# Tiles at multiples of 64 bytes, weights in block order from the host, float32 head transposes, and a new start of a two-layer diffusion backbone

## The chip, the cores and the metric

The kernel runs on one core of one Trainium2 chip, as one launch. The metric is device time in microseconds; three runs of the kernel before gave 1825.28, 1827.72 and 1827.8 us, the median is 1827.72 us. Beside these runs there is one profiled execution, from which all rows below come. TensorE is called PE, its loads of the stationary operand PEld, VectorE DVE, ScalarE ACT, GpSimd POOL, SyncE SP.

## The reference

Two layers over 256 latent and 256 context tokens of 1024 numbers in float32. Each layer is a half-step SwiGLU, a token mixing, and a half-step SwiGLU again, each with a modulation computed from a conditioning vector:

```python
# per layer; m = c_silu @ w_mod[l] + b_mod[l], nine rows of 1024 (shift, scale, gate of three parts)
h = rms_norm(x) * (1 + scale) + shift
x = x + 0.5 * gate * ((silu(h @ w_gate) * (h @ w_up)) @ w_down)          # D_FF = 2816
x = x + gate * mix(h)      # layer 0: windowed GQA with sink, and differential attention
                           # layer 1: latent attention (C) and 2-D neighbourhood attention (D)
x = x + 0.5 * gate * swiglu(h)
# in the mixings, per head: q, k = rope(rms_norm(q_or_k) * gain); softmax(q @ k.T) @ v
```

The last layer computes its last two parts for the latent tokens alone.

## The kernel before

Everything is kept transposed: `xT[k]` holds 128 channels by 512 tokens. A float32 product is made of three products in the float32r form: each operand is split into a high part and the rest (`split`, lines 97 to 99: an ACT copy and a DVE subtraction), and `mm3` issues hi·hi, hi·lo, lo·hi. In `mm(ps, a, b)` the first operand is the stationary one, the second the moving one.

**The four FFNs** (`ffn`). For each pair of 128-wide slices of D_FF, `wcols` loads 512 KB of weights into `raw`, four 128-row chunks of 256 columns (one row of a chunk is 1 KB in the weight matrix), and splits them into `hs`. The moving operands are `hT[0]` to `hT[7]`, the normed stream, two planes (hi, lo) of 512 tokens each; products land in `gps` and `ups`. Twelve matmuls of 512 columns belong to one slice and four chunks, and one product of gate or up of a pair has 48 in a row: for chunks 0 to 3, then for 4 to 7, both slices. The down projection has `ah` as moving operand and lands in `dps`. The fourth FFN has 258 columns, its moving operand is `hTl` with planes 264 floats apart. `residual` (line 294) adds the result to `xT`. In the last part `emit_out` transposes each finished `xT` on PE (`otp`, line 490), copies it and writes it out.

**The start.** Four tiles `xin` of tokens by channels are loaded, squared on ACT, transposed on PE (32 transposes into `xps`, line 557) to `xT`. `first_loads`, `first_mods` and `first_norm` work in four steps of two `hT` each: 2 MB of `w_mod` into `wm`, 64 matmuls `mps` (line 526; they run in float32, so the trace shows two for each instruction), a transpose `mpt`, then `hT`. The first pair of the first FFN is interleaved with these steps: its 96 matmuls want `hT` in order, and its two halves of weights.

**The mixings** are lists of items whose order is written out (`MIX0`, `MIX1`); a scheduler places the instructions of neighbouring items among each other. Twenty items call `head_rows` (18 with four heads, two with two): it norms and rotates q or k (`head_norm`, result `tk`), splits the result for both token blocks (`hsq`, `sp`), transposes the split heads (`trp`, line 661, 152 in all: per pair of heads four), and copies the result to a tile of 128 by 2 by 256, in which a head's hi part stands in partitions 0 to 63 and its lo part in 64 to 127 (lines 664 and 666). For keys a second tile with the halves exchanged is written (lines 669, 671, 673).

**Addresses.** Small constants share one tile, `const`, of 3636 floats, 14,544 bytes, which is 16 more than a multiple of 64. In the built program `const` itself (identity, ones, `cT`), `hT[0]` and `hT[1]` of the first two FFNs and `hT[0]` to `hT[3]` of the third one begin at multiples of 64 bytes; all other `hT`, every `hs`, `ah`, `hsq`, `tk` and most other tiles that TensorE reads begin 32 bytes behind one. In `hTl` the hi plane is at a multiple, the lo plane 32 behind.

Of the kernel before, what the change touches and what calls it, by code (L numbers as in the profile page):

```python
# [16 lines left out]
P = 128  # L17
# [45 lines left out]
def tile_hybrid_dit(ctx: ExitStack, tc: tile.TileContext, I, out, dbg=None):  # L63
# [74 lines left out]
    def const(name, shape, src=None):  # L138
# [3 lines left out]
        if name not in SHARED:  # L142
            place[name] = at, n
# [21 lines left out]
    bT = const("bT", [P, 2, 9, KC])  # L165
    brow = w2("brow")[:72, :256]
    Q.dma_start(out=brow.rearrange("n (l p) -> n l p", l=2), in_=I["b_mod"].rearrange("l (n p) -> n l p", p=P))

    S.activation(cvec, cvec, AF.Silu)
    cps = bank("tr", "cps")  # L170
    T.transpose(cps[:, :16], cvec, ident[:16, :16])
    for v in range(2):
        V.tensor_copy(cT[:, :, v], cps[:, 8 * v:8 * v + 8])
    bps = bank("tr", "bps")
    for l in range(2):
        T.transpose(bps[:, 72 * l:72 * l + 72], brow[:, l * P:(l + 1) * P], ident[:72, :72])
    V.tensor_copy(bT, bps[:, :144].rearrange("p (l m k) -> p l m k", l=2, m=9))
# [103 lines left out]
    xall = xp.tile([P, KC, NTOK], F32, tag="xT", name="xT")  # L281
    xT = [xall[:, k, :] for k in range(KC)]
# [200 lines left out]
    outs = {}  # L483

    def emit_out(dc):
        if dc % 4 == 0:
            outs["t"] = [w2(f"ot{b}") for b in range(2)]
        for b in range(2):
            pt = bank("tr", "otp")
            T.transpose(pt[:, :P], xT[dc][:, b * P:(b + 1) * P], ident)  # L490
            o = outs["t"][b][:, (dc % 4) * P:(dc % 4 + 1) * P]
            if b:
                S.copy(o, pt[:, :P])
            else:
# [7 lines left out]
    ss0 = const("ss0", [P, 4])
    xin = []
    for tb in range(4):
        t = up.tile([P, D], F32, tag="kq", name=f"xin{tb}", bufs=UNITS["kq"])
        src = I["x"][0] if tb < 2 else I["ctx"][0]
        Q.dma_start(out=t, in_=src[(tb % 2) * P:(tb % 2 + 1) * P, :])
        xin.append(t)


    def first_loads(q):
        tiles = {}
        for k0 in (0, 4):
            for m in (1, 0):
                t = up.tile([P, 4, 256], F32, tag="wm", name="wm", bufs=UNITS["wm"])
                c0 = m * D + 256 * q
                Q.dma_start(out=t, in_=I["w_mod"][0, k0 * P:(k0 + 4) * P, c0:c0 + 256].rearrange("(k p) f -> p k f", p=P))
                tiles[m, k0] = t
        return tiles

    def first_mods(q, tiles):
        ps = bank(("po", "md")[q % 2], "mps")
        for k in range(KC):
            for c in range(4):
                m, x = 1 - c // 2, c % 2
                T.matmul(ps[32 * c:32 * c + 32, :P], cT[:, k, :], tiles[m, k - k % 4][:, k % 4, P * x:P * x + P],  # L526
                         start=(k == 0), stop=(k == KC - 1), tile_position=(0, 32 * c))
        st = w2("mst")[:, :P]
        V.tensor_copy(st, ps[:, :P])
        pt = bank("tr", "mpt")  # L530
        T.transpose(pt[:, :P], st, ident)
        pv = pt[:, :P].rearrange("p (m x r) -> p m x r", m=2, r=32)
        for m in (1, 0):
            for v in range(2):
                add(modT[:, 0, v, m, 2 * q:2 * q + 2], pv[:, 1 - m, :, v], bT[:, 0, m, 2 * q:2 * q + 2])

    def first_norm(q):
        for k in range(2 * q, 2 * q + 2):
# [759 lines left out]
def consts():  # L1298
# [45 lines left out]
```

## Time and profile before

| what | value |
|---|---|
| median of three runs | 1827.72 us |
| profiled execution | 1823.43 us |
| its span, first to last instruction | 1821.4 us |
| mean granted TensorE clock | 0.994 |
| PE busy | 1771.1 us, 97% |
| PEld busy | 1537.0 us, 84% |
| DVE busy | 1219.5 us, 67% |
| ACT busy | 739.6 us, 41% |
| DMA | 256.90 MB, mean 141 GB/s |

A share is an average over stages: the start (0 to 57 us) is full of transfers, the FFNs (57 to 400, 647 to 1391, 1620 to the end) are full of matmuls, the mixings (400 to 647, 1391 to 1620) are where PE waits for other engines.

### The profile page before, as it was taken

How to read it: one execution, taken by the hardware profiler on the slowest of the kernel's cores; microseconds unless marked ns; L12 is line 12 of the kernel's file. 1: busy time of each engine (PE TensorE's matmuls, PEld its weight loads, DVE VectorE, ACT ScalarE, POOL GpSimd, SP SyncE). 2: the span in 40 equal slices, each digit the busy share in tenths (PEclk: the TensorE clock that was granted, in tenths of full speed). 3: DMA queues.
4: the chain of work that ended last, by engine and by line, in shares of the span. 5: the costliest groups of instructions: out<-in, count | busy, mean ns of one | idle time of the engine just before them, and what ended most of it. 6: DMA issues, size and time to landing. Idle time of an engine off the chain costs nothing.

```text
span 1821.4 us, 26782 instructions
## 1 busy us (share of the span) xinstructions
PE 1771.1 (97%) x10563; PEld 1537.0 (84%) x10563; DVE 1219.5 (67%) x2343; ACT 739.6 (41%) x1322; POOL 45.8 (3%) x25
## 2 busy tenths in 40 slices
PE   7999999999999989999999999999999998999999
PEld 5788888898998888888888988888889886789998
DVE  5999953467698699989944633333336688877564
ACT  4333132345666552322322332222234656664442
POOL 0000000011010000000000000000001011000000
PEclk9999999999999999999999999999999999999999
DMA  9877752322110137778943233333233442146552
GB/s 305 274 242 225 236 189 84 116 74 66 50 59 24 51 116 232 242 234 265 337 155 105 82 104 93 95 110 97 76 110 105 85 100 58 58 151 186 185 180 87
DMA packets 214026, 256.90 MB, mean 141 GB/s; under 512 B 21485, under 2 KB 195725, under 8 KB 213901
## 3 DMA queue, kind: packets, MB, share of 16 engines
q1 hardware_dynamic: 213900, 255.19, 45.4%
q8 instruction: 83, 1.36, 0.3%
q14 instruction: 43, 0.34, 0.1%
HBM read 254.11 MB, written 1.05 MB: 140 GB/s over the span
## 4 chain that ended last, share of the span: by engine, by line
PE 86%; DVE 7%; ACT 3%; DMA 2%; issue 1%; SPq 0%; ACTq 0%; DVEq 0%
PE ups L102 24%; PE gps L102 23%; PE dps L102 23%; PE ops L102 3%; PE po L758 2%; PE sc L102 2%; DVE hs L99 1%; DMA bias<-in_d_rpb_dram 1%; PE pdk L102 1%; PE paq L102 1%; PE trp L661 1%; PE ptl L726 1%; PE pdq L102 1%; ACT hs L98 1%; PE mps L526 1%
## 5 line engine op out<-in xcount | busy, mean ns | idle before, releaser
L99 DVE TENSOR_TENSOR hs<-raw,hs 128x1024 fp32r<-128x1024 f32 (+2 forms) x308 | 366.6, 1197 | 258.9 <-ACT hs L98 258.1
L98 ACT ACTIVATE hs<-raw 128x1024 fp32r<-128x1024 f32 (+2 forms) x308 | 314.3, 1030 | 498.2 <-PE dps L102 166.7
L102 PE MATMUL dps<-ah,hs 128*128 128x512 f32 (+1 forms) x2256 | 400.1, 338 | 0.2 <-DVE hs L99 0.2
L102 PEld LDWEIGHTS dps<-ah,hs 128*128 128x128 f32 x2256 | 350.6, 190 | 45.5 <-DVE hs L99 0.4
L102 PE MATMUL gps<-hT,hs 128*128 128x512 f32 (+1 forms) x1680 | 379.8, 382 | 5.6 <-ACT hT L544 2.6
L102 PE MATMUL ups<-hT,hs 128*128 128x512 f32 (+1 forms) x1680 | 377.7, 381 | 0.0
L102 PEld LDWEIGHTS gps<-hT,hs 128*128 128x128 f32 x1680 | 304.1, 189 | 71.0 <-ACT hT L544 3.5
L102 PEld LDWEIGHTS ups<-hT,hs 128*128 128x128 f32 x1680 | 304.6, 189 | 63.4 <-issue 1.0
L211 DVE CUSTOM_DVE_ANT_0 junk<-mraw,cb,const 128x1024 f32<-128x1024 f32 x224 | 283.1, 1281 | 14.0 <-DMA mraw<-in_k_w_modT_dram 8.3
L98 ACT ACTIVATE ah<-af 128x512 fp32r<-128x512 f32 (+1 forms) x88 | 50.5, 575 | 155.1 <-DVE af L92 121.9
L294 DVE SCALAR_TENSOR_TENSOR xT<-dps,const,xT 128x256 f32<-128x256 f32 x112 | 50.2, 478 | 86.2 <-PE dps L102 86.0
L92 DVE TENSOR_TENSOR af<-sg,ups 128x512 f32<-128x512 f32 x66 | 45.2, 685 | 62.5 <-PE ups L102 62.5
L275 POOL TENSOR_TENSOR hs<-raw,hs 128x1024 fp32r<-128x1024 f32 (+2 forms) x21 | 45.6, 2173 | 1566.0 <-ACT hs L274 1500.6
L430 ACT ACTIVATE sg<-gps 128x512 f32<-128x512 f32 x66 | 39.0, 591 | 91.4 <-PE gps L102 91.4
L102 PE MATMUL gps<-hTl,hs 128*128 128x258 f32 x528 | 66.8, 284 | 1.8 <-DVE hTl L375 1.0
L102 PEld LDWEIGHTS gps<-hTl,hs 128*128 128x128 f32 x528 | 64.7, 190 | 2.6 <-DVE hTl L375 1.2
L102 PE MATMUL ups<-hTl,hs 128*128 128x258 f32 x528 | 65.5, 283 | 0.0
L102 PEld LDWEIGHTS ups<-hTl,hs 128*128 128x128 f32 x528 | 64.4, 190 | 0.0
L99 DVE TENSOR_TENSOR ah<-af,ah 128x512 fp32r<-128x512 f32 (+1 forms) x88 | 54.5, 620 | 13.3 <-ACT ah L98 13.3
L686 DVE TENSOR_REDUCE nm<-sc 128x1 f32<-128x512 f32 (+1 forms) x80 | 53.8, 682 | 5.1 <-PE sc L102 4.8
L692 ACT ACTIVATE pr<-sc,nm 128x512 f32<-128x512 f32 (+1 forms) x64 | 40.4, 635 | 18.6 <-DVE nm L686 16.6
L303 ACT ACTIVATE sq<-xT 128x256 f32<-128x256 f32 (+1 forms) x54 | 24.0, 450 | 53.5 <-DVE xT L294 53.0
(296 smaller groups left out, 1892.5 us busy)
## 6 DMA issues: line engine op xcount, KB each, us to landing
mraw<-in_k_w_modT_dram SPq DMA_DIRECT2D x128, 512.0 KB, 4.7
raw<-in_ffn_w_gate_dram SPq DMA_DIRECT2D x88, 512.0 KB, 4.8
raw<-in_ffn_w_up_dram SPq DMA_DIRECT2D x88, 512.0 KB, 4.3
raw<-in_ffn_w_down_dram SPq DMA_DIRECT2D x80, 512.0 KB, 3.6
raw<-in_cd_w_in_dram SPq DMA_DIRECT2D x18, 512.0 KB, 3.9
wm<-in_w_mod_dram SPq DMA_DIRECT2D x16, 512.0 KB, 8.9
raw<-in_ab_w_in_dram SPq DMA_DIRECT2D x16, 512.0 KB, 3.7
raw<-in_ffn_w_down_dram SPq DMA_DIRECT2D x16, 256.0 KB, 2.8
```

What stands on the lines that cost most here:

```text
L92: V.tensor_tensor(out=out_, in0=a, in1=b, op=ALU.mult)
L98: S.activation(h, src, AF.Copy)
L99: V.tensor_tensor(out=l, in0=src, in1=h.bitcast(F32), op=ALU.subtract)
L102: T.matmul(ps, a, b, start=start, stop=stop)
L211: V.tensor_tensor_reduce(out=junk, in0=raw, in1=mod_c[v], scale=0.5 if m in (2, 8) else 1.0, scalar=bT[:, l, m, k:k + 1], op0=ALU.mult, op ...
L275: nc.gpsimd.tensor_tensor(out=hs[:, 1, :n], in0=raw[:, :n], in1=hs[:, 0, :n].bitcast(F32), op=ALU.subtract)
L294: V.scalar_tensor_tensor(out=xT[dc][:, a:e], in0=ps[:, a:e], scalar=modT[:, l, v, m, dc:dc + 1], in1=xT[dc][:, a:e], op0=ALU.mult, op1=ALU ...
L303: S.activation(sq[:, cols], xT[dc][:, cols], AF.Square)
L430: S.activation(sg, g[:, :ntok], AF.Silu)
L686: V.tensor_reduce(out=nm[:, c], in_=view, axis=AX.X, op=ALU.max, negate=True)
L692: S.activation(p[:, cols], sc[:, cols], AF.Exp, bias=nm[:, i + b:i + b + 1], accum_out=den[:, i + b:i + b + 1])
L758: T.matmul(po[64 * x:64 * x + 64, q], val(x, c), pts[x][c], start=c == order[0], stop=c == order[-1], tile_position=(0, 64 * x))
```

## The change

Operands: `const` slots are rounded up to 16 floats, the tile has 3808 floats (15,232 bytes, 238 times 64), and the planes of `hTl` are 272 floats apart. In the built program every operand that TensorE reads then begins at a multiple of 64 bytes.

Layout: the host hands over the stream and the conditioning transposed, `b_mod` transposed, the FFN weights, `ab_w_in`, `ab_w_out`, `cd_w_out` and the first two rows of `w_mod` in blocks, so that a partition's part of a 512 KB load is one run of 4 KB. `cd_w_in`, `w_uq`, `w_ukv` stay. The output is written transposed from `xT`, and the host turns it.

Start: no `xin`, no `xps`; squares are taken from `xT` and summed on DVE; the modulation comes in five steps (one, one, two, two, two `hT`), and all loads of `w_mod` are issued ahead of the second half of the first pair's weights.

Head rows: `tk` is transposed in float32, two heads in one transpose (76 in place of 152), and the split is done behind the transpose: per head an ACT (or DVE) copy of 64 partitions and a DVE subtraction; the exchanged key tile is copied from the first, four copies in place of two.

```diff
-NCONST = 3636
+NCONST = 3808
...
-            place[name] = at, n
+            place[name] = at, -(-n // 16) * 16
...
     def wcols(w, k0, nk, c0, nw, tag=None):
         n = nk * nw
-        src = w[k0 * P:(k0 + nk) * P, c0:c0 + nw].rearrange("(k p) f -> p k f", p=P)
+        if len(w.shape) == 4:
+            assert nw == 256 and c0 % 256 == 0
+            src = w[c0 // 256, :, k0:k0 + nk, :]
+        else:
+            src = w[k0 * P:(k0 + nk) * P, c0:c0 + nw].rearrange("(k p) f -> p k f", p=P)
...
-            hraw.append(hp.tile([P, KC, 2, 264], R32, tag="hTl", name="hTl", bufs=1))
+            hraw.append(hp.tile([P, KC, 2, 272], R32, tag="hTl", name="hTl", bufs=1))
...
     def emit_out(dc):
-        if dc % 4 == 0:
-            outs["t"] = [w2(f"ot{b}") for b in range(2)]
-        for b in range(2):
-            pt = bank("tr", "otp")
-            T.transpose(pt[:, :P], xT[dc][:, b * P:(b + 1) * P], ident)
...
+        Q.dma_start(out=out[dc * P:(dc + 1) * P, :], in_=xT[dc][:, 0:256])
...
+    STEPS = ((0, 1), (1, 1), (2, 2), (4, 2), (6, 2))
+
+    wmall = [up.tile([P, 2, 2, D], F32, tag="wm", name="wm", bufs=4) for _ in range(4)]
...
+    for k in range(KC):
+        if k == 0:
+            S.activation(ssum, xT[k], AF.Square)
+        else:
+            xsq = wmall[3].rearrange("p a m f -> p (a m f)")[:, NTOK * k:NTOK * k + NTOK]
+            S.activation(xsq, xT[k], AF.Square)
+            add(ssum, ssum, xsq)
+    first_mods(*STEPS[0], wms[0])
...
+    def first_steps(b):
+        if b == 0:
+            wms[1:] = [first_loads(*step) for step in STEPS[1:]]
+        for i in ((1, 2), (3, 4))[b]:
+            first_mods(*STEPS[i], wms[i])
+            first_norm(*STEPS[i])
...
     def head_rows(src, v, gain, rope, idm, dst_of, swap_of=None):
...
-            split(spv[:, :, 0, :].bitcast(R32), spv[:, :, 1, :].bitcast(R32), tv[:, b])
-            spf.append(sp)
+        pt = bank("tr", "trp")
         for i in range(nh // 2):
-            pt = bank("tr", "trp")
+            for b in range(2):
+                T.transpose(pt[:, 256 * i + b * P:256 * i + (b + 1) * P], tk[:, (b * nh + 2 * i) * HD:(b * nh + 2 * i + 2) * HD],
+                            idm)
+        for i in range(nh // 2):
+            d = dst_of(i)
             for x in range(2):
-                for b in range(2):
-                    h = 2 * i + x
-                    T.transpose(pt[:, 256 * x + b * P:256 * x + (b + 1) * P], spf[b][:, P * h:P * h + P], idm)
...
+                own, other = (slice(0, 64), slice(64, 128))[::1 - 2 * x]
+                r = pt[own, 256 * i:256 * i + 256]
+                if now[0] in ROWS_DVE.split():
+                    V.tensor_copy(d[own, x], r)
+                else:
+                    S.activation(d[own, x], r, AF.Copy)
+                V.tensor_tensor(out=d[other, x], in0=r, in1=d[own, x].bitcast(F32), op=ALU.subtract)
```

How the scheduler places this, at three places. First the queue of SP at the start of the program, before (a name ending in `_dram` is an input; `wm` is `w_mod`, `raw` an FFN's weights):

```order
L149 DMA const<-in_k_ident_dram 128x128
L167 DMA brow<-in_b_mod_dram 72x2x128
L507 DMA xin_106<-in_ctx_dram 128x1024
L517 DMA wm<-in_w_mod_dram 128x4x256 x4
L268 DMA raw<-in_ffn_w_gate_dram 128x4x256
L268 DMA raw<-in_ffn_w_up_dram 128x4x256
L517 DMA wm<-in_w_mod_dram 128x4x256 x8
L268 DMA raw<-in_ffn_w_gate_dram 128x4x256
L268 DMA raw<-in_ffn_w_up_dram 128x4x256
L517 DMA wm<-in_w_mod_dram 128x4x256 x4
```

and now:

```order
L161 DMA xT<-in_k_xT_dram 128x1024
L493 DMA wm<-in_k_wm_dram 128x1024
L265 DMA raw<-in_k_ffn_w_gate_dram 128x1024
L150 DMA const<-in_k_ident_dram 128x128
L265 DMA raw<-in_k_ffn_w_up_dram 128x1024
L493 DMA wm<-in_k_wm_dram 128x1024 x2
L499 DMA wm<-in_k_wm_dram 128x1024 x12
L265 DMA raw<-in_k_ffn_w_gate_dram 128x1024
L265 DMA raw<-in_k_ffn_w_up_dram 128x1024
L191 DMA cb<-in_c_dram 128x1024
```

The second half of the first pair's weights moved behind the last four of the sixteen loads of `w_mod`; it is now the last of the 24 large transfers of the start.

Second, PE where the first matmul of the FFN stands, before (`nbc` is the norm's broadcast) and now (there it is called `bcs`):

```order
L102 MATMUL nbc<-dg,const 128x128
L526 MATMUL mps<-wm,const 32x128 x16
L102 MATMUL nbc<-dg,const 128x128
L526 MATMUL mps<-wm,const 32x128 x7
L531 MATMUL mpt<-const,mst 128x128
L102 MATMUL gps_472<-hT,hs 128x512
```

```order
L508 MATMUL mps<-wm,const 32x128 x13
L103 MATMUL bcs<-dg,const 128x128 x2
L508 MATMUL mps<-wm,const 32x128 x3
L103 MATMUL bcs<-dg,const 128x128
L514 MATMUL mps<-wm,const 32x128
L103 MATMUL bcs<-dg,const 128x128
L519 MATMUL mpt<-const,mst 128x128
L514 MATMUL mps<-wm,const 32x128 x9
L103 MATMUL gps_423<-hT,hs 128x512
```

Before, the first `gps` stands behind the modulation of the first two `hT`; now it stands behind the first `mps` of the third step too, which read the thirteenth of the 24 transfers.

Third, PE at the first call of `head_rows` in the first mixing (the rows of `bq00`; `pbk` and `pbv` are projections that the scheduler puts around it), before and now:

```order
L102 MATMUL pbk<-hs,hT 128x256 x69
L102 MATMUL pbv<-hw,hT 128x256 x15
L102 MATMUL pbk<-hs,hT 128x256 x2
L102 MATMUL pbv<-hw,hT 128x256
L661 MATMUL trp<-const,hsq 128x128 x2
L102 MATMUL pbv<-hw,hT 128x256
L661 MATMUL trp<-const,sp 128x128
L661 MATMUL trp<-const,hsq 128x128
L661 MATMUL trp<-const,sp 128x128 x2
L661 MATMUL trp<-const,hsq 128x128
L661 MATMUL trp<-const,sp 128x128
```

```order
L103 MATMUL pbk<-hs,hT 128x256 x68
L103 MATMUL pbv<-hw,hT 128x256 x5
L650 MATMUL trp<-const,tk 128x128 x4
L103 MATMUL pbk<-hs,hT 128x256
L103 MATMUL pbv<-hw,hT 128x256 x7
L103 MATMUL pbk<-hs,hT 128x256 x2
```

Eight transposes became four, they read `tk` itself, and they stand some 14 matmuls earlier.

## Rows read from the trace of the kernel before

**Rows 1.** The page: busiest engine, and the chain that ended last, by engine.

```profile
PE 1771.1 (97%) x10563; PEld 1537.0 (84%) x10563; DVE 1219.5 (67%) x2343; ACT 739.6 (41%) x1322; POOL 45.8 (3%) x25
...
PE 86%; DVE 7%; ACT 3%; DMA 2%; issue 1%; SPq 0%; ACTq 0%; DVEq 0%
```

**Rows 2.** PE's groups by shape: line, tiles, count | busy us, mean ns | idle before.

```profile
L102 PE MATMUL gps<-hT,hs 128*128 128x512 f32 x1488 | 351.0, 393 | 3.8 <-ACT hT L544 2.6 <-DVE hs L99 1.2
...
L102 PE MATMUL dps<-ah,hs 128*128 128x512 f32 x1152 | 262.6, 389 | 0.0
...
L490 PE MATMUL otp<-const,xT 128*128 128x128 f32 x16 | 3.7, 290 | 0.5 <-DVE xT L294 0.5
```

**Rows 3.** PE in stretches of the third FFN: length, busy (instructions), clock, DMA.

```profile
1102.29:1107.89 5.60, 5.60 (x25) 1.00 0.31 95
1107.89:1113.37 5.48, 5.48 (x26) 1.00 0.29 86
```

**Rows 4.** PE's timeline in its down projection: start, length, tiles, count.

```profile
1157.69 47.53 PE L102 MATMUL dps<-ah,hs 128*128 128x512 f32 x209
```

**Rows 5.** Stretches before and in the second mixing: length, PE, PEld, DVE, ACT, POOL, clock, DMA.

```profile
1022.22:1025.05 2.83, 2.83 (x26) 2.83 (x25) 2.69 (x5) 0.83 (x2) 0.00 (x0) 1.00 0.61 185
1396.60:1398.02 1.42, 1.42 (x15) 1.42 (x13) 0.59 (x1) 1.22 (x2) 1.42 (x1) 1.00 0.54 186
1398.02:1399.46 1.44, 1.44 (x14) 1.44 (x13) 1.41 (x3) 0.73 (x3) 0.94 (x1) 1.00 0.01 4
```

**Rows 6.** Timeline of PE, ACT and DVE where the second pair begins.

```profile
56.31 1.17 PE L102 MATMUL gps<-hT,hs 128*128 128x512 f32 x4
56.62 1.06 ACT L98 ACTIVATE hs<-raw 128x1024 fp32r<-128x1024 f32 x1
...
57.37 1.22 DVE L99 TENSOR_TENSOR hs<-raw,hs 128x1024 fp32r<-128x1024 f32 x1
58.64 5.60 PE L102 MATMUL gps<-hT,hs 128*128 128x512 f32 x23 [1.16 <-DVE hs L99]
```

**Rows 7.** Stretches with full DMA: 1 KB runs, then mostly 4 KB runs (last columns: share, GB/s).

```profile
2.40:42.00 39.60, 30.81 (x294) 21.63 (x295) 21.23 (x68) 17.67 (x30) 0.00 (x0) 1.00 1.06 345
112.00:116.00 4.00, 4.00 (x19) 3.26 (x18) 3.96 (x7) 1.06 (x1) 0.00 (x0) 1.00 0.98 363
```

**Rows 8.** PE's transposes of one call of head_rows, as a stretch.

```profile
572.46:573.25 0.79, 0.79 (x8) 0.79 (x8) 0.00 (x0) 0.04 (x1) 1.00 0.08 21
```

**Rows 9.** DVE's and ACT's groups of head_rows, and a split out of PSUM.

```profile
L99 DVE TENSOR_TENSOR hsq<-tk,hsq 128x256 fp32r<-128x256 f32 x18 | 8.9, 497 | 1.9 <-ACT hsq L98 1.9
L99 DVE TENSOR_TENSOR sp<-tk,sp 128x256 fp32r<-128x256 f32 x18 | 7.5, 417 | 0.0
...
L99 DVE TENSOR_TENSOR ckt<-cktr,ckt 96x256 fp32r<-96x256 f32 x16 | 6.1, 413 | 0.7 <-ACT ckt L98 0.6
...
L673 DVE CAST dkt<-trp 64x512 fp32r<-64x512 f32 x6 | 4.1, 684 | 4.0 <-ACT dkt L669 4.0
...
L98 ACT ACTIVATE hsq<-tk 128x256 fp32r<-128x256 f32 x18 | 7.5, 414 | 19.4 <-DVE tk L92 9.9 <-DVE tk L95 9.5
```

**Rows 10.** The two mixings as stretches (columns as in the fifth group).

```profile
400.48:647.15 246.67, 237.03 (x1819) 216.94 (x1817) 193.60 (x501) 154.15 (x376) 12.51 (x6) 0.99 0.19 56
1390.88:1619.53 228.65, 212.57 (x1495) 185.13 (x1493) 175.03 (x445) 142.67 (x348) 23.29 (x11) 0.98 0.36 88
```

**Rows 11.** What PE waited for: us in total, times, longest.

```profile
PE trp L661 <- DVE hsq L99: 7.8, 6, 2.5
PE kvt L1109 <- DVE ckv L1105: 4.8, 1, 4.8
```

**Rows 12.** The end: timeline of all engines.

```profile
1817.12 0.48 DVE L294 SCALAR_TENSOR_TENSOR xT<-dps,const,xT 128x256 f32<-128x256 f32 x1 [0.23 <-PE dps L102]
...
1818.14 0.27 ACT L493 COPY ot<-otp 128x128 f32<-128x128 f32 x1 [0.45 <-PE otp L490]
1818.35 0.81 SPq L498 DMA_DIRECT2D out_dram<-ot  x2
```

More of the change, by code (lines that the diff above doesn't have):

```diff
@@ L164, in tile_hybrid_dit @@
     modT = const("modT", [P, 2, 2, 9, KC])
[L165 to L177, printed above, removed]
+    bT = const("bT", [P, 2, 9, KC], I["k_bT"])
+    S.activation(cT[:, :, 0:2], cvec, AF.Silu)
     for m0 in (1, 2):
@@ L502, in tile_hybrid_dit @@
[L502 to L518, printed above, removed]
-        return tiles
@@ L521, in first_mods @@
[L521 to L527, printed above, removed]
+        Q.dma_start(out=out[dc * P:(dc + 1) * P, :], in_=xT[dc][:, 0:256])
+    STEPS = ((0, 1), (1, 1), (2, 2), (4, 2), (6, 2))
@@ new lines, in first_mods @@
+    def first_mods(j, nj, tiles):
+        ps = bank("po", "mps")
+        if nj == 1:
+            for k in range(4):
+                for c in range(4):
+                    T.matmul(ps[32 * c:32 * c + 32, :P], cT[:, k + 4 * (c % 2), :], tiles[1 - c // 2][k + 4 * (c % 2)],
+                             start=(k == 0), stop=(k == 3), tile_position=(0, 32 * c))
+        else:
+            for k in range(KC):
+                for c in range(4):
+                    x = c % 2
+                    T.matmul(ps[32 * c:32 * c + 32, :P], cT[:, k, :], tiles[1 - c // 2][k][:, P * x:P * x + P],
+                             start=(k == 0), stop=(k == KC - 1), tile_position=(0, 32 * c))
@@ L533, in first_mods, with first_norm @@
         for m in (1, 0):
[L534 to L538, printed above, removed]
+            if nj == 1:
+                half = sml(2, "mh")
+                V.tensor_scalar(out=half, in0=pv[:, 1 - m, 0, 0:2], scalar1=bT[:, 0, m, j:j + 1], scalar2=None, op0=ALU.add)
+                add(modT[:, 0, :, m, j], pv[:, 1 - m, 1, 0:2], half)
+            else:
+                for v in range(2):
+                    add(modT[:, 0, v, m, j:j + 2], pv[:, 1 - m, :, v], bT[:, 0, m, j:j + 2])
+    def first_norm(j, nj):
+        for k in range(j, j + nj):
             t = unit("xn", "xn")
@@ L812, in mix0 @@
     def mix0():
-        w_in, w_out = I["ab_w_in"][0], I["ab_w_out"][0]
+        w_in, w_out = I["k_ab_w_in"][0], I["k_ab_w_out"][0]
         tabs = {}
@@ L1267, in w @@
     def w(l, n):
-        return [I[f"ffn{n}_w_{x}"][l] for x in ("gate", "up", "down")]
-    def first_steps(b):
-        for q in ((1, 2), (3,))[b]:
-            first_step(q)
+        return [I[f"k_ffn{n}_w_{x}"][l] for x in ("gate", "up", "down")]
     mixing = [mix0(), mix1()]
@@ L1321, in consts, with laid_out, blocks @@
     return c
-_OUT = (SEQ, D)
+_OUT = (D, SEQ)
+def laid_out(a):
+    import numpy as np
+    a = {k: np.asarray(v) for k, v in a.items()}
+    def blocks(w):
+        n, k, f = w.shape
+        return w.reshape(n, k // P, P, f // 256, 256).transpose(0, 3, 2, 1, 4)
+    c = {"k_xT": np.concatenate([a["x"][0], a["ctx"][0]]).T.reshape(KC, P, NTOK).transpose(1, 0, 2),
+         "k_cT": np.stack([a["c"][0], a["c_ctx"]]).reshape(2, KC, P).transpose(2, 1, 0),
+         "k_bT": a["b_mod"].reshape(2, 9, KC, P).transpose(3, 0, 1, 2),
+         "k_wm1": a["w_mod"][0, :, :2 * D].reshape(KC, P, 2, KC, P)[:, :, :, :2].transpose(3, 2, 1, 0, 4),
+         "k_wm0": a["w_mod"][0, :, :2 * D].reshape(KC, P, 2, 4, 256).transpose(3, 2, 1, 0, 4)}
+    for nm in ("ab_w_in", "ab_w_out", "cd_w_out", *(f"ffn{n}_w_{x}" for n in (1, 2) for x in ("gate", "up", "down"))):
+        c["k_" + nm] = blocks(a[nm])
+    return c
 def kernel(**inputs):
```

115 lines of the change are left out of this document (53 added, 62 removed).

## The prediction

> **What bounds the kernel now.** I read the page first: PE is busy for 97% of the span and holds 86% of the chain that ended last [rows 1]. So a gain must come out of the matmuls themselves, out of the few places where PE waits, or out of the two ends of the program. Then I took PE's groups by shape: most of its time is wide matmuls, 1488 recorded for `gps`, about as many for `ups`, and 1152 for `dps` [rows 2]. Their pace is not one number. In one product of the third FFN the first 24 matmuls read `hT[0]` to `hT[3]`, at a multiple of 64 bytes, against `hs`, 32 bytes behind one, and took 5.60 us; the next 24, both operands at 32, took 5.48 [rows 3], with the clock at 1.00 in both. In a down projection, where `ah` and `hs` are both at 32, 209 took 47.53 us [rows 4]; taking 0.39 us as the length of one [rows 2] off the end, that is (47.53 - 0.39) / 208 = 0.2266 us from start to start. So 24 at the best pace are 5.44 us. Unequal offsets go with 0.16 us more for 24, or 6.8 ns each, and the block behind them with another 0.04. Third, stretches of the mixings, where PE is idle for 246.7 - 237.0 = 9.6 us and 228.7 - 212.6 = 16.1 us [rows 10], and the table of waits for whom it waits. Last, timelines of the two ends.
>
> **Alignment.** If equal offsets are what matters, (0, 0) is as good as (32, 32). A product of the third FFN then gains (5.60 + 5.48) - 2 x 5.44 = 0.20 us; in the first two, half of the unequal matmuls (`hT[0]`, `hT[1]`) gain 0.08 + 0.04 = 0.12. With two products for each of ten full pairs in each FFN: 20 x 0.20 + 40 x 0.12 = 8.8 us. The trace holds no wide product with both operands at a multiple of 64, so this is bounded: 0 if it behaves as now, 8.8 if as (32, 32). I take 8.8, since the blocks differ in nothing that I can see but the offset. At 256 columns the sign is the other way: in the second mixing twelve matmuls with unequal offsets took 1.42 us, the following twelve with equal ones 1.44 [rows 5]; some 670 of the mixings' projections are unequal now, so 670 x 1.7 ns = 1.1 us are lost. Together -7.7.
>
> The Trainium skill, "TensorE: Matmul & The Clock Gate", section "Step-by-step: what each phase is for", says that the moving operand and the weight load have separate read ports and that the next load takes nothing from the running matmul. By that no offset of one against the other should count, and this term would be 0. The rows disagree by 0.12 us in 24 matmuls.
>
> **Start.** The first pair does not wait for PE: with 100 matmuls done at 58.64 us, 96 were done, at 0.227 each, by 57.7 in effect; the wait of 1.16 us before is for the second pair's `hs` [rows 6]. The transfers run at 345 GB/s from 2.4 to 42 us, in runs of 1 KB [rows 7]. Runs of 4 KB, which the FFNs' `mraw` has already, reached 363 [rows 7], so the layout gives 0 to 5% there and I count nothing for it. What shortens the start is order and work: 24 transfers of 0.524 MB and 0.2 MB of small ones are 12.8 MB, in 37.1 us at 345 GB/s, so the last, the second half of the first pair's `up`, lands at 39.5 us (37.7 at 363). ACT's copy of 1.06 and DVE's subtraction of 1.22 us [rows 6] lie behind it, partly under matmuls on `gate`, which lands one transfer earlier (0.524 MB at 345 GB/s, 1.5 us): PE begins the last 48 matmuls near 40.3 and ends them 10.9 us later, at 51.2. Gain: 57.7 - 51.2 = 6.5 us. A wait for the second pair's weights may follow, as now. I take -6, between -3 (a wait of three such) and -8 (363 GB/s).
>
> **Head rows, PE.** Eight transposes take 0.79 us as PE goes through them [rows 8], so 76 fewer save 7.5. The moved split also frees what PE waits for: `trp` waits 7.8 us in six waits for `hsq`, the split [rows 11], and ACT's 0.41 and DVE's 0.50 of it [rows 9] no longer stand ahead of it. Six waits shorter by 0.9 are 5.4; not every release will come that early, since `tk` itself is late, so I take -3 (0 to -5.4).
>
> **Head rows, DVE.** Gone: 36 splits, 8.9 + 7.5 = 16.4 us [rows 9], 0.9 for four of half width, sixteen copies of 0.684 (five of rows, eleven of swaps), 10.9; 28.2 in all. New: 76 subtractions of 256 columns out of PSUM, by the nearest row (`ckt`, 0.413 [rows 9]) 31.4 us; ten row copies at the same price, 4.1; 22 swaps at half of 0.684, 7.5; 43.0 in all. DVE does 14.8 us more, and has 193.6 of 246.7 and 175.0 of 228.7 us full [rows 10]. ACT does less, since the 36 split copies of 0.4 us go and its row copies stay about as long. DVE's new work stands between the transposes and the scores (`sc`), but PE has projections to do in between, and the waits of the mixings that are not from this chain (`kvt`, 4.8 us [rows 11]) stay. Bounds: 0, if projections cover all, to 14.8, if PE waits for each. I take a third, +4.9: the cover is there in the first mixing, and in the second it is thinner. Mixings together: -7.5 - 3 + 4.9 = -5.6.
>
> **Tail.** Sixteen `otp` leave PE: at the pace of the other transposes 1.6 us, a pair by itself takes longer (2 x 0.29 at most [rows 2]), so I take 2.0. Behind the last `residual` (ends 17.60) stood a transpose and a copy, ended at 18.41, before the output's DMA [rows 12]; now the DMA follows directly: 0.8. Together -2.8 (0.8 to 3: all `otp` but the last pair may lie in gaps).
>
> **Sum.** -7.7 - 6 - 5.6 - 2.8 = -22.1 against the profiled execution's 1823.4 gives 1801.3. The median of the runs is 1827.7, higher by a factor of 1.0024; so 1805.5.
>
> **The rivals.** *The offset is not the cause.* Then the alignment term falls to 0, by rows 3 unlikely, as the two blocks differ in the chunk too but nothing else in the trace makes chunks 0 to 3 slower: 1805.5 + 7.7 = 1813. The rule on the two read ports in "TensorE: Matmul & The Clock Gate" of the Trainium skill would lead here. *DVE sets the pace in the mixings.* With DVE at 78% there, the whole 14.8 us lands as waits of `sc` for the rows; for it speaks that the keys' three steps (rows, subtraction, swap) are now in series, against it that PE waits little on this chain now: 1805.5 + 9.9 = 1815. *The multiple of 64 is the slow one, of the other sign.* In all slow blocks the moving operand stood at a multiple of 64. If that alone costs 6.8 ns, the change puts every wide matmul there: 60 products x 48 x 6.8 ns = 19.6 us over the best pace instead of 8.8 now, and 1152 `dps` x 6.8 ns = 7.8. Against the forecast that is 8.8 + 10.8 + 7.8 = 27.4 us: 1833, slower. It decides as soon as the start and the mixings give less than 18.6 us together. Against it speaks that at 256 columns 24 `gps` with the moving `hT[0]` to `hT[3]` at a multiple of 64 took 2.83 us, 118 ns each, no slower than the twelve of the second mixing whose moving `hs` stood at 32 and whose stationary `hT` at 0, 1.42 us [rows 5]. *Better than forecast.* All of the waits for `hsq` go, DVE's work is covered, 4 KB runs hold 363 GB/s: 1805.5 - 2.4 - 4.9 - 2 = 1796, or less where the second pair's waits go as well.
>
> **How the numbers follow.** Forecast 0.55, own range 1796 to 1812; offset not the cause 0.10; DVE 0.19; moving operand at 64 slow 0.07; better 0.09. The range of 1790 to 1820 leaves out the third rival and some of two adding up. About 0.2% (3.7 us) is what a measurement of this kernel can tell from no change; from that, slower 0.06 (the third rival, less the cases where the rest covers it), same 0.07 (its milder form, or the first two rivals with a start that gives nothing), faster 0.87.
>
> **What would show it.** Alignment: in the third FFN both blocks of 24 at 5.44 us, and `dps` unchanged at 0.2266; both at 5.60 and `dps` at 0.2334 would be the third rival. Start: the second pair's `gps` beginning near 52 us. Head rows: 76 `trp` at about 0.1 us, the waits for `hsq` gone; if DVE is the bound, the list of waits shows `sc` released by DVE's subtraction or swap, and the idle time of PE in the mixings grows beyond 26 us. Tail: the last DMA issued right behind the last `xT`. The prediction is wrong if the start's transfers do not hold 345 GB/s, or if the 256-column matmuls change by more than their 1.7 ns, since there are thousands of them.

## The result, and the profile after

The changed kernel takes 1839.47 us (median of four runs, 1838.33 to 1839.88), the kernel before 1827.13 us beside it: a ratio of 1.0069, 95% interval 1.0056 to 1.0082. It is slower by 12.3 us where 22 us less were forecast, and outside the range. The profiled executions differ by 15.2 us in their spans (1836.6 and 1821.4).

First the page of the changed kernel, busiest engines and the chain that ended last, by engine:

```profile
PE 1775.0 (97%) x10445; PEld 1529.0 (83%) x10445; DVE 1243.6 (68%) x2390; ACT 733.1 (40%) x1327; POOL 45.8 (2%) x25
...
PE 83%; DVE 11%; ACT 3%; DMA 1%; issue 1%; SPq 0%; DVEq 0%; ACTq 0%
```

PE's share of the chain fell from 86 to 83%, DVE's rose from 7 to 11% [rows 1]: PE waits for DVE more often. But PE is busy for longer too, with fewer instructions.

Which matmuls, a product of the third FFN shows (PE in stretches of 24; length, busy and count, clock, DMA share, GB/s):

```profile
1306.11:1311.57 5.46, 5.46 (x26) 1.00 0.39 107
1311.57:1317.14 5.57, 5.57 (x25) 1.00 0.27 87
```

and the timeline of its down projection:

```profile
1172.63 67.36 PE L103 MATMUL dps<-ah,hs 128*128 128x512 f32 x288
```

Every operand here begins at a multiple of 64 bytes, and still one block is slow, now the second. The two blocks together are no faster than before by more than 0.05 us (11.03 and 11.08 us [rows 3]). The down projection, untouched by the plan, went from 0.2266 to (67.36 - 0.39) / 287 = 0.2333 us [rows 4].

The start, PE's timeline at four places, then SP's at the load of the first pair's second half:

```profile
21.25 1.19 PE L103 MATMUL bcs<-dg,const 128*128 128x128 f32 x4 [2.57 <-DVE dg L559]
...
26.56 0.73 PE L103 MATMUL gps<-hT,hs 128*128 128x512 f32 x2 [0.20 <-ACT hT L537]
...
47.94 0.74 PE L103 MATMUL gps<-hT,hs 128*128 128x512 f32 x2 [0.81 <-DVE hs L100]
...
58.30 2.01 PE L103 MATMUL gps<-hT,hs 128*128 128x512 f32 x8
```

```profile
39.01 0.33 SPq L265 DMA_DIRECT2D raw<-in_k_ffn_w_gate_dram  x1
```

and two stretches of it (length, PE, PEld, DVE, ACT, POOL, clock, DMA share, GB/s):

```profile
4.00:30.00 26.00, 15.15 (x143) 10.17 (x147) 14.82 (x45) 8.54 (x15) 0.00 (x0) 1.00 1.03 407
31.00:39.00 8.00, 8.00 (x89) 5.46 (x89) 3.93 (x15) 1.82 (x4) 0.00 (x0) 1.00 0.12 46
```

Before, the first `gps` stood at:

```profile
22.00 1.38 PE L102 MATMUL gps<-hT,hs 128*128 128x512 f32 x4 [1.79 <-ACT hT L544]
```

The second pair begins at 58.30 us, 0.6 later than the 57.7 in effect before [rows 6]; forecast was 51.2. (Before, the first pair's own 96 matmuls had ended at 56.31, the start of the four `gps` in [rows 6], which are the second pair's; the wait of 1.16 us behind them is now gone.) The transfers were faster than forecast, 407 GB/s against 345 [rows 7], and then stood nearly still from 31 to 39 us while PE was busy throughout.

The two mixings as stretches, and what PE's transposes of the heads waited for:

```profile
405.04:659.43 254.39, 236.02 (x1767) 212.26 (x1765) 209.44 (x533) 153.62 (x386) 12.34 (x6) 0.99 0.18 55
1408.05:1638.14 230.09, 212.29 (x1470) 183.22 (x1469) 182.26 (x464) 143.20 (x356) 23.61 (x11) 0.97 0.35 88
```

```profile
PE trp L650 <- DVE tk L96: 5.0, 3, 2.6
PE trp L650 <- DVE tk L93: 4.4, 5, 1.7
...
PE trp L650 <- DVE nm L685: 1.4, 1, 1.4
```

They are 7.7 and 1.4 us longer than before [rows 10], with DVE busier by 15.8 and 7.2 us. PE is idle for 18.4 and 17.8 us in them, 36.2 together against 25.7 before; beyond 26 us was the prediction's sign that DVE is the bound, but what waits is `trp` for `tk`, and hardly `sc` for the rows. `trp` waits 10.8 us in these three rows, where it waited 7.8 us for `hsq` [rows 11].

The end looks as forecast (timeline of DVE and SP, the output's DMA right behind `xT`):

```profile
1832.78 1.05 SPq L479 DMA_DIRECT2D out_dram<-xT  x2
1832.98 0.48 DVE L289 SCALAR_TENSOR_TENSOR xT<-dps,const,xT 128x256 f32<-128x256 f32 x1 [0.23 <-PE dps L103]
```

From the second mixing's end to the span's end it was 201.9 us before (1821.4 - 1619.53) and is 198.5 now.

So the 15.2 us stand, with the second pair's begin and the ends of the mixings [rows 6, 10] as marks: start +0.6; first FFN from there to the mixing +4.0; first mixing +7.7; second and third FFN, 748.6 against 743.7, +4.9; second mixing +1.4; fourth FFN and tail -3.4.

### The profile page after: what moved, and what is told of

Read it like the earlier page. It is cut to its first block, busy times and chain, and to the rows that moved or that the text cites. A ratio compares the mean times of both kernels' runs of the same rounds, so it can differ in the third digit from the quotient of the medians.

```text
span 1836.6 us, 26561 instructions
## 1 busy us (share of the span) xinstructions
PE 1775.0 (97%) x10445; PEld 1529.0 (83%) x10445; DVE 1243.6 (68%) x2390; ACT 733.1 (40%) x1327; POOL 45.8 (2%) x25
## 3 DMA queue, kind: packets, MB, share of 16 engines
q1 hardware_dynamic: 95728, 255.19, 43.9%
## 4 chain that ended last, share of the span: by engine, by line
PE 83%; DVE 11%; ACT 3%; DMA 1%; issue 1%; SPq 0%; DVEq 0%; ACTq 0%
PE ups L103 23%; PE gps L103 23%; PE dps L103 23%; PE ops L103 2%; PE po L755 2%; DVE hs L100 2%; PE sc L103 1%; DVE nm L683 1%; PE pcq L103 1%; DVE tk L93 1%; PE pdk L103 1%; PE ptl L723 1%; PE pdq L103 1%; DVE hT L349 1%; DVE ht L93 1%
## 5 line engine op out<-in xcount | busy, mean ns | idle before, releaser
L103 PE MATMUL dps<-ah,hs 128*128 128x512 f32 (+1 forms) x2256 | 405.0, 340 | 0.0
L204 DVE CUSTOM_DVE_ANT_0 junk<-mraw,cb,const 128x1024 f32<-128x1024 f32 x224 | 283.8, 1281 | 15.7 <-DMA mraw<-in_k_w_modT_dram 11.6
L100 DVE TENSOR_TENSOR ah<-af,ah 128x512 fp32r<-128x512 f32 (+1 forms) x88 | 54.6, 621 | 13.3 <-ACT ah L99 13.3
```

What stands on the lines that cost most here:

```text
L100: V.tensor_tensor(out=l, in0=src, in1=h.bitcast(F32), op=ALU.subtract)
L103: T.matmul(ps, a, b, start=start, stop=stop)
L204: V.tensor_tensor_reduce(out=junk, in0=raw, in1=mod_c[v], scale=0.5 if m in (2, 8) else 1.0, scalar=bT[:, l, m, k:k + 1], op0=ALU.mult, op ...
```

## The experiments

All times are medians; the kernel before took 1826.9 to 1827.9 us beside them.

### Offsets: the constants' tile at 3712 floats, in the changed kernel

The slow block gives the clue. In the built program of the changed kernel, `hs` begins mostly at 128 modulo 512 bytes, `hT[0]` to `hT[3]` at 128 too, `hT[4]` to `hT[7]` and `ah` at 0. In the kernel before, `hs`, `ah` and `hT[4]` to `hT[7]` were all at 352, `hT[0]` at 128. The fast blocks are those with equal offsets modulo 512, not modulo 64. One size mends all of them: 3712 floats are 29 times 512 bytes.

```diff
-NCONST = 3808
+NCONST = 3712
...
-            place[name] = at, -(-n // 16) * 16
+            place[name] = at, n
```

> The changed kernel with one size changed: the tile of the constants has 3712 floats (29 times 512 bytes) and its slots are packed without rounding, so that nearly every wide pair (all of hT with hs, ah with hs, the projections) has moving and stationary operand at the same offset modulo 512 bytes. Theory A (a wide matmul is slow where the two offsets differ modulo 512 or 256 bytes, whatever they are modulo 64): dps falls from 232.7 to 226.7 ns from start to start, gps and ups from 231.1 to about 227.5; 1224 x 6.0 ns + 3168 x 3.6 ns = 18.7 us, so about 1821 us. Theory B (a moving operand at a multiple of 64 bytes is slow by itself): all operands stay at multiples of 64, so dps stays near 233 and the time at 1839 us.

Measured: 1819.89 us, 19.6 less than the changed kernel, ratio to before 0.9957 (0.9944 to 0.9971). In the built programs PE's first 9155 of some 10,220 instructions stand in the same order in both, so it is the addresses that differ. Two blocks of 24 in its third FFN, and a down projection:

```profile
1093.06:1098.50 5.44, 5.44 (x26) 1.00 0.30 102
1098.50:1103.94 5.44, 5.44 (x26) 1.00 0.25 91
```

```profile
1158.34 65.44 PE L103 MATMUL dps<-ah,hs 128*128 128x512 f32 x288
```

Both blocks are at the best pace of [rows 4], with every moving operand at a multiple of 64. Theory B, the prediction's third rival, falls. By the same marks as above, the first three FFNs are some 18 us shorter than in the changed kernel and 9.3 us shorter than before.

### The same size in the kernel before

```diff
-NCONST = 3636
+NCONST = 3712
```

> The kernel before with the tile of the constants at 3712 in place of 3636 floats and nothing else. That moves hs, ah and hT[2] to hT[7] from 352 to 128 modulo 512 bytes, where hT[0] and hT[1] are already. Theory A (equal offsets modulo 512 count): gps and ups fall from 230.5 to about 227.5 ns, dps stays at 226.7; 3168 x 3.0 ns = 9.5 us, less 1 us for the 256-column pairs that lose their odd offset: about 1818.5 us. Theory B (a moving operand at a multiple of 64 is slow): every wide matmul goes to 233 ns, about +15 us, 1842 us.

Measured: 1818.94 us, ratio 0.995 (0.9937 to 0.9963). Blocks of its third FFN, in the place of the 5.60 and 5.48 of before:

```profile
1110.18:1115.62 5.44, 5.44 (x25) 1.00 0.36 110
1115.62:1121.06 5.44, 5.44 (x25) 1.00 0.29 98
```

One number gives 8.4 us. What the change was after in this part was there to be had, by another rule.

### Pairs of offsets by themselves

The kernel's matmuls are these alone; `dm` and `dw` are the offsets in bytes:

```python
for j in range(48):
    m = 1024 * (j % 8) + dm // 4
    w = 512 * (j % 8) + dw // 4
    T.matmul(ps[:, :cols], wgt[:, w:w + P], mov[:, m:m + cols], start=(j == 0), stop=(j == 47))
```

> Not the kernel's computation: only float32r matmuls on one tile of data, in 37 blocks of 48, each block with one pair of byte offsets (moving, stationary) on top of bases that are equal modulo 512; 512, 384 and 256 columns. It leaves out everything else and writes zeros. Theory A with a period of 512 or 256 bytes: blocks of 512 columns with equal offsets take 226.7 ns a matmul at 0, 32, 64 and 128; with a difference of 32, 64, 96, 128, 160, 192 or 224 about 231 to 235; with 512 it is 226.7 again, and 256 tells whether the period is 256 or 512. The reverse sign (stationary shifted) the same. At 256 columns differences cost nothing (118 to 120 ns). Theory B: moving offset of a multiple of 64 slow (0, 64, 128 at 233), 32 fast, whatever the stationary one.

Blocks of 48 as PE's stretches. The pairs (moving, stationary) in bytes are, in order: (32, 32), (128, 128), (16, 0), (32, 0), (64, 0), (128, 0), (256, 0), (512, 0), (0, 128) with 512 columns; (0, 0) and (128, 0) with 384; (0, 0), (32, 0) and (256, 0) with 256.

```profile
23.86:34.77 10.91, 10.91 (x49) 1.00 0.01 2
45.67:56.60 10.93, 10.93 (x49) 1.00 0.00 0
67.49:78.61 11.12, 11.12 (x50) 1.00 0.00 0
78.61:89.81 11.20, 11.20 (x49) 1.00 0.01 1
89.81:100.80 10.99, 10.99 (x50) 1.00 0.00 0
112.01:123.20 11.19, 11.19 (x49) 1.00 0.01 1
156.83:167.71 10.88, 10.88 (x49) 1.00 0.00 0
178.91:189.81 10.90, 10.90 (x50) 1.00 0.00 0
212.20:223.36 11.16, 11.16 (x50) 1.00 0.00 0
267.21:275.55 8.34, 8.34 (x49) 1.00 0.00 0
292.19:300.63 8.44, 8.44 (x49) 1.00 0.00 0
308.95:314.70 5.75, 5.75 (x50) 1.00 0.01 3
314.70:320.36 5.66, 5.66 (x51) 1.00 0.00 0
331.71:337.46 5.75, 5.75 (x50) 1.00 0.00 0
```

With 512 columns a matmul takes 226.7 to 227.7 ns (10.88 to 10.93 us / 48) where the two offsets are equal modulo 256: also at a difference of 256 or 512, and whatever the common offset is. With the moving operand ahead by 16 bytes it costs 5 ns more, by 32 or 128 6.5, by 64 only 2.3. The sign changes little at 32 and 128, but at 64 it does: (0, 64) takes 11.20 us for 48, 6.6 ns more for each. At 256 columns the order is reversed: 120 ns with equal offsets, 118 with a difference of 32. At 384 a difference of 128 cost 2 ns; of 32 and 64, nothing. Nothing else ran beside these blocks (DMA share 0.00 to 0.01), so it is the two operands alone. The period is 256 and not 512, which the kernels could not tell.

### Head rows as before

In the changed kernel, `head_rows` alone is the old one (the change's lines on it reversed; the core of it):

```diff
-            for b in range(2):
-                T.transpose(pt[:, 256 * i + b * P:256 * i + (b + 1) * P], tk[:, (b * nh + 2 * i) * HD:(b * nh + 2 * i + 2) * HD],
-                            idm)
...
+            split(spv[:, :, 0, :].bitcast(R32), spv[:, :, 1, :].bitcast(R32), tv[:, b])
...
+                    T.transpose(pt[:, 256 * x + b * P:256 * x + (b + 1) * P], spf[b][:, P * h:P * h + P], idm)
```

> The changed kernel with head_rows as before (split ahead of the transposes, four transposes for two heads, one copy for rows and two for the swap), all else as changed. Theory C (the new order of work costs PE idle time in the mixings because DVE does 15 us more there; PE's idle time rose by 8.7 us in the first and 1.7 us in the second mixing, the clock took 3.2 us more): the mixings go back to near 247 and 229 us, so 1839.5 - 9 = about 1830 us, with PE idle near 10 and 16 us. Rival (the mixings are slower for another reason: operands' offsets, loads in another layout, the later start): idle time stays, and 76 transposes more cost 7 us: about 1846 us.

Measured: 1826.8 us, 12.7 less than the changed kernel; the gain was larger than expected. The new `head_rows` is a loss of that size, though it has half the transposes.

### Both mended

> The changed kernel with both parts mended that the first runs pointed to: constants' tile of 3712 floats, so that wide pairs have equal offsets modulo 256 bytes, and head_rows as before. If the two are independent: 1826.8 - (1839.5 - 1819.9) = about 1807 us, dps at 226.7 ns, mixings near 246 and 224 us. Rival: part of one is in the other (the mixings' waits come from slower projections), so the sum is smaller: 1812 us or more.

Measured: 1807.64 us, ratio 0.9891 (0.9878 to 0.9905), faster than both kernels, and the two parts add up (19.6 and 12.7 us). Its mixings, and below them those of e1, which has the new `head_rows`:

```profile
398.63:644.03 245.40, 236.56 (x1819) 217.36 (x1817) 193.91 (x501) 154.31 (x376) 12.64 (x6) 0.99 0.18 56
1379.90:1604.30 224.40, 211.40 (x1495) 183.89 (x1494) 175.00 (x445) 142.56 (x348) 23.23 (x11) 0.98 0.37 91
```

```profile
399.00:652.30 253.30, 237.14 (x1766) 214.40 (x1764) 209.35 (x533) 153.56 (x386) 12.30 (x6) 0.98 0.18 54
1389.50:1619.10 229.60, 210.60 (x1470) 181.47 (x1469) 182.09 (x464) 143.22 (x356) 23.33 (x11) 0.98 0.35 89
```

PE's busy time in each is the same within 0.8 us in spite of 76 transposes (7.5 us) less: the granted clock was at 0.50 for 20.5 us of these stretches in e1 and for 10.2 in e5, and half of the difference, 5.1 us, is busy time that fills most of what the transposes left; the other 2 us stay unexplained. PE's idle time (length less busy time) is 8.8 and 13.0 us with the old, 16.2 and 19.0 with the new `head_rows`. DVE is busy for 22.5 us more; the operations that were exchanged account for 15.4 of it.

### Is it VectorE's load? Four runs

First, e5 (old `head_rows`) with added load:

```diff
+            V.tensor_tensor(out=sq[0:64, 0:256], in0=pt[0:64, 0:256], in1=tk[0:64, 0:256], op=ALU.subtract)
             if swap_of is not None:
                 d = swap_of(i)
```

> As e5 (old head_rows), with one more VectorE subtraction of 64 partitions by 256 columns out of PSUM for each pair of heads (38 in all, 0.41 us each, 15.7 us), whose result nothing reads: the load that the new head_rows adds to VectorE, and not the longer chain. Theory C1 (VectorE's load makes the waits): idle time of PE in the mixings rises from 22 to about 35 us and the clock falls more often, 1817 to 1823 us. Theory C2 (it is the chain of transposes, copy, subtraction and swap behind each other that is late): at most 3 us more, 1808 to 1811 us.

Measured: 1820.53 us, 12.9 more than e5. Its mixings:

```profile
398.40:647.60 249.20, 237.11 (x1819) 217.70 (x1817) 200.71 (x527) 152.89 (x376) 12.23 (x6) 0.99 0.18 55
1384.60:1619.10 234.50, 215.38 (x1495) 186.31 (x1493) 181.80 (x457) 142.02 (x348) 23.11 (x11) 0.97 0.35 88
```

So 15.7 us of DVE work whose result nothing reads cost four fifths of their length, though DVE was busy for only some 80% of these stretches. PE's idle time in them is 31.2 us, 9.4 more than in e5, and the clock was at 0.50 for 17.1 us in place of 10.2, which loses another 3.4. The loss lies mostly in the second mixing, whereas the new `head_rows` loses more in the first: the load is not the whole likeness. Nor is it the load alone that was added: DVE stood still for 4.8 us ahead of these operations, mostly for ACT's copies (the second row is e12, the next run, where it was 2.7 us, for PE's transposes), and the scheduler's order is not quite that of e5 either.

```profile
L665 DVE TENSOR_TENSOR hsq<-trp,tk 64x256 f32<-64x256 f32 x38 | 15.7, 414 | 4.8 <-ACT bkt L664 1.7 <-ACT dkt L664 1.3 <-ACT bqt L664 0.5
L665 DVE TENSOR_TENSOR hsq<-tk 64x256 f32<-64x256 f32 x38 | 15.7, 414 | 2.7 <-PE trp L659 2.5
```

These additions also read PSUM and keep its bank, as the new subtractions do. In the next run they read SBUF instead (both operands are `tk[0:64, 0:256]`):

> As e10 (1820.5 us), but the 38 added VectorE subtractions read the normed heads in SBUF in place of the transposes in PSUM, at the same place (they overwrite the split that the transposes have read) and of the same size, so that they hold no PSUM bank. Theory F1 (VectorE's time itself delays what the projections and scores wait for): again 1817 to 1822 us. Theory F2 (the added reader keeps the transposes' PSUM bank longer, and the next call's transposes wait for the bank; the new head_rows does that too): close to e5, 1807.5 to 1811 us.

Measured: 1815.32 us, 7.7 above e5; between the two theories. About six tenths of the price, half the length of the added work, stay without the read of PSUM; the rest went with that read, or with the order that the scheduler then chose (its order changed in all engines' queues).

Then, in e1, work taken off DVE. Row and swap copies on ACT:

```diff
-SWAP_ACT = """dk01 bk11 bk00 ak0"""
-ROWS_DVE = """bv11 uq0 bq00 dq10 bv01 ak0 uk10 cq00"""
+SWAP_ACT = """bk00 bk01 bk10 bk11 ak0 ak1 dk00 dk01 dk10 dk11"""
+ROWS_DVE = ""
```

> The kernel of e1 (new head_rows, constants at 3712 floats, 1819.9 us) with all row copies and all swap copies of head_rows on ACT: 32 operations, about 11 us, leave DVE; ACT gets about 10 us more. Theory C1 (DVE's load makes the waits in the mixings): idle time of PE in the mixings falls from 35 by several us, 1813 to 1817 us. Theory C2 (the chain is longer whichever engine does it: transpose, copy, subtraction, swap in series behind each other, and transposes wait for tk): within 1.5 us of 1819.9 us, or slower since ACT's copies now stand in series.

Measured: 1829.17 us, 9.3 more than e1. And 29 weight splits on GpSimd, by more names in the list `POOL`:

```diff
-POOL = """of21 od30 of20 oa01 dk00 dv10 uq1 bk11 uk00 oa20 bq00 oa30 aq11 uk01 ob30 ob10 dq00 bk10 oc20 dv11 ob31 oa00
+POOL = """bk01 bv00 bq01 bq10 bv01 bv10 ak1 aq00 aq10 cq00 cq10 cq20 dk11 dk01 dq10 dv00 ckv0 uq0 uk10 uk11
+    of21 od30 of20 oa01 dk00 dv10 uq1 bk11 uk00 oa20 bq00 oa30 aq11 uk01 ob30 ob10 dq00 bk10 oc20 dv11 ob31 oa00
```

> As e1 (new head_rows, 1819.9 us), with the subtraction of 29 more weight splits of the mixings on GpSimd in place of VectorE: about 32 us of work leave VectorE there, more than the new head_rows added; the chain of head_rows stays. Theory C1 (VectorE's load): PE's idle time in the mixings falls from 35 to 20 to 25 us, 1805 to 1812 us. Theory C2 (the chain): little changes, 1817 to 1823 us, or slower where a matmul waits for GpSimd's subtraction, which takes twice as long.

Measured: 1835.17 us, 15.3 more than e1, with `trp` waiting for `tk` as the largest of PE's waits in the mixings:

```profile
PE trp L651 <- DVE tk L94: 10.0, 6, 2.9
```

DVE's busy time in the mixings was only about 8 us less here than in e1, and PE waited longer. The splits that left DVE had taken 31.4 us in e1; but 115 DVE operations now overlapped GpSimd's subtractions, and they took 32.3 us more than the median of their kind (in e1 42 of them, 21.6 us). GpSimd's subtractions took 2.2 us each, where DVE's had taken 1.1. So this run hardly lightened DVE, and says little on Theory C1. In e8 DVE was busy for 11.9 us less and PE waited longer all the same: there Theory C1 in its plain form, that DVE's sum of work makes the waits, does not hold. What is shown is that added DVE work was paid with half (e12) to four fifths (e10) of its length, and that these two moves did not buy it back.

### The start: three runs

All from e5, so 1807.6 us is what they stand against. In the first, `mst` takes a small tile of its own, since in the changed kernel SP waited 16.4 us for a transpose that reads an `mst` which lies in a raw buffer's bytes:

```diff
-        st = w2("mst")[:, :P]
+        st = small.tile([P, P], F32, tag="dg", name="mst", bufs=2)
```

> As the run before, with one edit: the copy of a modulation step (mst) takes a small tile of its own instead of one that shares its bytes with the third raw buffer, so that SP's load of the first pair's second half of weights no longer waits 16.4 us for the last but one transpose of the modulation (39.0 us in the changed kernel) and is issued near 23 us. Theory D (from the first gps at 26.6 us on the start is bound by PE's own work, 96 wide matmuls and the modulation's, and by the chain to the first hT): the weights come 8 us or more earlier and the pair ends at most 0.8 us earlier (its one wait for hs), so 1806 to 1807 us. Theory E (the prediction's: the last transfer of the start sets the end of the first pair): the pair ends 5 to 6 us earlier, 1801 us.

Measured: 1808.81 us; but SP issued the load no earlier, at 40.94 us, because the new tile was again put into the raw buffers' bytes. The run says nothing on the question. The next does what it should have done:

```diff
-        st = w2("mst")[:, :P]
+        st = ssum[:, P * (j // 2):P * (j // 2) + P] if j else w2("mst")[:, :P]
```

> As e5 (1807.6 us), with the copies of the last four modulation steps (mst) in the tile of the squares' sum, which is free by then, so that nothing that shares bytes with the raw buffers is alive and SP's loads of the first pair's second half need not wait for PE: what e6 was meant to do and did not (there SP still waited 11.2 us for mpt and issued them at 40.9 us). Theory D (PE's own work bounds the start from the first gps on): the loads are issued some 10 us earlier, the first pair ends at most 0.8 us earlier (57.8 in place of 58.6 us), 1806.8 us. Theory E (the last transfer sets the end): 5 us earlier, 1802 us.

Measured: 1806.88 us. SP's issues and PE's first matmul of the second pair:

```profile
29.75 0.39 SPq L265 DMA_DIRECT2D raw<-in_k_ffn_w_gate_dram  x1
30.93 0.33 SPq L265 DMA_DIRECT2D raw<-in_k_ffn_w_up_dram  x1
```

```profile
58.37 11.04 PE L103 MATMUL gps<-hT,hs 128*128 128x512 f32 x48
```

Loads ten microseconds earlier (in e5 the first was issued at 39.62), the pair's end at 58.37 in place of 58.60 us: Theory D. The last of the three has the first two weight splits' subtractions on GpSimd:

```diff
+    wcalls = []
...
+        wcalls.append(0)
-        if now[0] and now[0] in POOL.split():
+        if len(wcalls) <= 2 or now[0] and now[0] in POOL.split():
```

> As the first of these four, with the subtractions of the first two weight splits (the first pair's first half) on GpSimd in place of VectorE, where they stand with 1.22 us each inside the chain of small operations that makes the norm's factor. Theory D: the first gps comes about 2.4 us earlier (24 in place of 26.6 us) if GpSimd's subtractions (2.2 us each) are done by then, and the end of the first pair with it: 1804.5 us. Theory E: no change, 1807 us.

Measured: 1810.56 us. The first `gps` came earlier, at 25.26 in place of 26.74 us, and the second pair later:

```profile
25.26 1.65 PE L103 MATMUL gps<-hT,hs 128*128 128x512 f32 x3
...
61.59 2.66 PE L103 MATMUL gps<-hT,hs 128*128 128x512 f32 x11
```

Behind the first `gps` now stood 192 records of `mps` in place of 172, and more waits: the scheduler moved modulation work behind it. So Theory D's price for an earlier first matmul is not shown; it holds only if the same work stays ahead of it.

## Why the prediction was wrong, step by step

**Alignment, forecast -7.7 (-8.8 in the FFNs, +1.1 in the mixings), measured +8.9 in the first three FFNs** (4.0 + 4.9). The step that failed is the use of "If equal offsets are what matters, (0, 0) is as good as (32, 32)" for this change, with offsets counted modulo 64, and the choice of the full 8.8 us on it. Equal offsets are what matters at 512 columns, but modulo 256, and the change made them equal modulo 64 only: in the built program 1152 of the 1224 wide `dps` have offsets that differ by 128, where before none differed. That (0, 0) is as good was even true, at 10.88 us for 48 in e4, and so was the size: with equal offsets the three FFNs are 9.3 us shorter than before (e1). I read the offset in 64 bytes off the change's words and off two blocks that fit it; the same blocks fit 128, 256 and 512 as well, and the addresses in the built program would have told that the change puts `ah` and half of `hT` 128 bytes away from `hs`. The third rival had the price of the slow matmuls nearly right (`dps` at 0.2333 us; its 6.8 ns is 6.7 by its own rows, 0.16 us / 24) by the wrong mechanism: a moving operand at a multiple of 64 is fast in e1.

At 512 columns a matmul took 226.7 ns with equal offsets and 233.3 at a difference of 32 bytes (e4). The Trainium skill says in "TensorE: Matmul & The Clock Gate", section "Step-by-step: what each phase is for", that the next load of weights takes no read bandwidth from the running matmul. By that the offset of one against the other should not count; the measurement says that it does. That it is the load of the weights that disturbs the matmul is not shown: no run changed the offset of one without a load of the other.

The 1.1 us that equal offsets should lose at 256 columns rest on a pace that e4 confirms, 120 against 118 ns. But the change did not make these offsets equal: 2354 of 3840 matmuls of 256 columns have unequal ones in its built program, 720 before.

**Start, forecast -6, measured +0.6.** The failed step is "the last, the second half of the first pair's `up`, lands at 39.5 us", taken as what ends the pair. It landed later than that, behind SP's wait, and did not matter (e9). What I left out is PE's own work: from the first `gps` on, PE is busy without a break of a microsecond in both kernels, with 96 matmuls and the modulation's. And the first `gps` came at 26.6 instead of 22.0 us; ahead of it stands the norm's factor, which now needs the summed squares of all `xT`, `st`, a dozen small DVE operations with two weight splits among them, and `bcs`. How much each costs is not shown; without the two splits on DVE the first `gps` came 1.5 us earlier (e7). The layout's gain, counted as nothing, was real (407 GB/s) and was not on the path.

**Head rows, forecast -5.6, measured +9.2 in the two mixings.** DVE's work was sized well: in e1's profile the 76 subtractions take 0.42 us each, and the whole 43.9 us against 43.0 forecast. The failed step is "I take a third, +4.9". The second rival, that all of it lands, was nearer but fell short too: with the other two terms it gives -7.5 - 3 + 14.8 = +4.3 us for this part, and the net loss was 9.2 in the profiles and 12.7 in e3. The term of `trp`'s waits failed as well: they did not fall by 3 us but rose, from 7.8 to 10.8, and the last that they wait for is `tk` itself, no longer the split. Why `tk` is late is not shown; in e10, with as much DVE work more, `trp`'s wait for `hsq` stayed at 8.1 us (7.9 in e5). The transposes' 7.5 us are a saving of busy time, and the sum had no term for the clock: PE waited 13.3 us more in e1 than in e5, and the lower clock lost 5.1 us more.

**Tail, forecast -2.8, measured -3.4** with the fourth FFN, whose own pace is in it; no run separates the two.

Alignment and heads were wrong in sign, by 17.7 (in the FFNs) and 14.8 us; the start missed by 6.6. One run mended the alignment part (e1), one the heads (e3), both together gave 1807.6: near the forecast's 1805.5, but by chance, with other terms than it had.

What stays open is how the new `head_rows`' price divides between DVE's time, its waits for ACT's copies, the PSUM bank that its readers hold and the order that the scheduler builds: e12 separates 7.7 from 12.9 us, but its order differs too. That the new `head_rows` as a whole costs 12 to 13 us is shown (e3, and e1 against e5); that DVE's load is the cause is shown only in part.

## What to carry to other kernels

When matmuls of one shape run at two paces, list the addresses of both operands for each pace from the built program, modulo every power of two up to 1024, before believing an alignment rule; then try one size. Count work that moves onto an engine at 80% as paid for until a run shows otherwise, even where PE seems to have other things to do (here added work cost half to four fifths of its length), and halving an operation on the busiest engine can be worth nothing where that engine then waits. And before a transfer is called the end of a stage, add up what the consumer still has to do from its first instruction on.

## What the hardware showed that was not expected

The dependence on the offset modulo 256 bytes, its reversal at 256 columns and its near absence at 384 (all in e4). Transfers with runs of 4 KB reached 407 GB/s over 26 us where runs of 1 KB gave 345 over 40. DVE's operations became longer where they overlapped GpSimd's (e11). And the granted clock fell to its lower level of 1.2 GHz after some waits of PE: in the changed kernel after two of 1.44 and 0.54 us close together (from 569.4 on) as well as after one of 2.60, but not after one of 2.19 (at 543.0). This is the one of 2.60 us, in the first mixing, before `trp` at 434.69:

```profile
434.69 0.63 PE L650 MATMUL trp<-const,tk 128*128 128x128 f32 x4 [2.60 <-DVE tk L96]
```

```profile
435.48:438.89 3.41, 3.41 (x18) 3.41 (x17) 2.61 (x7) 3.26 (x10) 0.00 (x0) 0.50 0.50 190
438.89:445.00 6.11, 6.11 (x54) 6.11 (x53) 3.73 (x7) 5.84 (x14) 2.40 (x1) 1.00 0.01 3
```

The stretch has the clock at 0.50, then it is 1.00 again; 3.41 us at half speed lose 1.7 us. So a wait in the mixings can cost more than its own length.
